# A hybrid decoder step on one core: a ragged tile spread over four row strips, and expert rows gathered at another pace

## The chip, the cores and the metric

The kernel runs on one core of a Trainium2 chip. The metric is the device time of one execution in microseconds, median of three runs. A profiled execution is kept beside them; its rows name the engines PE (TensorE, with PEld for its weight loads), DVE (VectorE), ACT (ScalarE), POOL (GpSimd) and SP (SyncE).

## The reference, cut to what matters

One layer of a decoder over 336 tokens: 256 prompt tokens, 8 sequences of 8 new tokens, and 16 meta tokens that stand ahead of the prompt.

```
proj = rmsnorm(x) @ w_in + b_in
... Conformer branch: GLU, depthwise conv of width 31, layernorm, silu, @ w_conf_out
... Mamba-2 branch: depthwise conv of width 4, then for each chunk of a segment
    acs   = cumsum(dt * A)
    y     = (C B^T * exp(acs_t - acs_s), causal) @ (dt * x)  +  C h * exp(acs)
    h_new = exp(acs_last) * h + B^T @ (exp(acs_last - acs) * dt * x)
... gated group norm over 8 groups, @ w_m_out
x = x + (g_a * y_a + g_b * y_b) @ w_o
# product-key experts, for each token and each of 8 heads
s1, i1 = top_k(q1 @ keys1, 16);  s2, i2 = top_k(q2 @ keys2, 16)
sc, f  = top_k(all 256 sums s1 + s2, 16);  ids = 128 * i1[f // 16] + i2[f % 16]
w      = softmax(sc) * gelu(U[ids] . x)
x      = x + sum over the 128 picks of w * V[ids]
```

Segments are the 16 meta tokens, two chunks of 128 prompt tokens, and each sequence's 8 tokens. The outputs are the normed tokens and the new caches and states.

## The kernel before, in words

**Projections.** Tokens stand along the free dimension (`T` = 336, `T2` = 320 without the meta tokens). Each block of 128 output features is three times eight matmuls over a split of weight and activation into a high and a low part (`proj`, L159 for every recorded matmul `mm`). `weight` fetches 512 KB on the SP queue, ACT makes the high part `wh` and POOL the low part `wl`.

**State-space groups.** There are eight groups; `ssd(g, ...)` is a generator whose steps are run between the projections of the next group by a list written out by hand, and the order on TensorE is that of the program (`keep_in_program_order`). Tokens are cut into three tiles (`TILES`): two prompt chunks of 128, and one tile of 80 rows: eight sequences of 8 rows and the 16 meta rows. `turn` transposes a tile of x and B, `inner` makes the scores of a tile within itself, `state` the running prompt state (for the meta tokens from rows 64 to 80), `running` the part that comes from the old states, `out` sums up a half of the features, and `update` adds to the eight sequences' states in `st`: B is multiplied by four masks (`Bm`), 32 rows hold four sequences, and each of two calls makes four matmuls of 32 rows into two PSUM banks (one of tag `misc`, one of tag `pj`). A group's sum of squares is brought to row g of an eight-row PSUM tile by a stationary of 8 columns from `gsel` (`pgn`).

**Expert stage.** 16 projections `w_q` give queries; for each the scores `psc` of three token tiles (`KTILES`: 128, 128 and 64 tokens) are matmuls with the query as the stationary operand. DVE sorts them (`top16`), tile 0 first. Tile 0 and the 8 last sample tokens get their expert rows by indirect DMA: `gather` brings one row of U and V (8 KB) for each of 128 partitions into one of five buffers `wuv`; 136 such gathers make 136 picks, each a dot product (L1207), two ACT steps and a weighted sum (L1215). The other 184 tokens are done densely: 128 blocks of U (`u_block`, L1284, 16 recorded matmuls a block) and then 128 blocks of V (`v_block`, L1378), 512 KB each on the SP queue, through a ring of eight slots. Between them `g_step` (one-hot matmuls, L1312) scatters the softmax weights.

**Order in that stage.** `Feed` deals tasks out over the blocks: sorting tasks of tiles 1 and 2 and picks over the first `SB` = 84 U blocks, then picks and one-hot steps. `NU` = (42, 28, 37) says how many picks go to U blocks 0 to 83, to the other 44, and to V blocks 0 to 63; the rest goes to the last V blocks. `place` transposes the sorted places of tile 1 and tile 2 on TensorE; `PLACE` = (38, 50) are the U blocks behind which they may stand. Here the order on the engines is the scheduler's, but for such bounds. A gather waits for an earlier block through a list:

```
steps = ustep[SB:] + vstep
if len(steps) > LEAD:
    tc.add_manual_dep(i_.ins, steps[-1 - LEAD], ...Sync...)
```

`ustep` and `vstep` name the first or last matmul of the blocks written so far and `LEAD` is 4, so gathers written among the first 84 U blocks wait for no block.

Of the kernel before, what the change touches and what calls it, by code (L numbers as in the profile page):

```python
# [22 lines left out]
PJ = 512  # L23
# [32 lines left out]
NU = (42, 28, 37)  # L56
# [9 lines left out]
PLACE = (38, 50)  # L66
# [34 lines left out]
NCK = CST["tri"][0]  # L101
NCM = CST["suf"][0]


def constants():
    c = np.zeros((128, NCST), np.float32)

    def put(name, a):
        o, n = CST[name]
        c[:a.shape[0], o:o + n] = a  # L110

    i = np.arange(128)
    put("ident", np.eye(128))
    put("tri", i[:, None] <= i[None, :])
    put("suf", i[:, None] > i[None, :])
    s = np.concatenate([np.arange(64) // 8, np.full(16, 8)])
    j = np.arange(80)
    same = s[:, None] == s[None, :]
    put("tri3", same & (j[:, None] <= j[None, :]))
    put("suf3", same & (j[:, None] > j[None, :]))  # L120
    put("seg", s[:, None] == np.arange(9)[None, :])
    put("segs", i[:, None] % 32 // 8 == np.arange(4)[None, :])
    put("gsel", np.broadcast_to(np.eye(8).reshape(1, 64), (128, 64)))
    for q in range(NQ):
        for t in range(TS):
            c[32 * (q % 4) + 8 * (q // 4) + t, CST["selq"][0] + 8 * q + t] = 1.0
    put("ones", np.ones((128, 128)))
    put("iota128", np.broadcast_to(np.arange(128), (128, 128)))
    put("sel32", i[:, None] % 32 == np.arange(32)[None, :])
    put("sel16", i[:, None] % 16 == np.arange(16)[None, :])  # L130
    put("sel8", i[:, None] % 8 == np.arange(8)[None, :])
    return c


def causal():
    m = np.zeros((128, T), np.float32)
    i, j = np.arange(128), np.arange(80)
    s = np.where(j < 64, j // 8, 8)
    m[:80, 256:] = np.where((s[:, None] == s[None, :]) & (j[:, None] <= j[None, :]), 0.0, -1e30)
    for t0 in (0, 128):  # L140
        m[:, t0:t0 + 128] = np.where(i[:, None] <= i[None, :], 0.0, -1e30)
    return m


def body(tc, ia, oa, stop=None):
    nc = tc.nc
    with ExitStack() as top:
# [220 lines left out]
        dt = dp.tile([H, T], F32, name="dt")  # L368
        dta = dp.tile([H, T], F32, name="dta")
# [39 lines left out]

        def step_sizes():  # L410
# [4 lines left out]
            nc.vector.tensor_scalar(dta, dt, aexp, -1.0, op0=OP.mult, op1=OP.mult)  # L415
            yield
            for i, (t0, L) in enumerate(TILES):
                p = ps.tile([128, 2 * H], F32, name="pdt2", tag="y", bufs=2) if i == 0 else misc([128, 2 * H], "pdt2")
                tr(p[:L, :H], dt[:, t0:t0 + L], ident[:H, :H])
                tr(p[:L, H:], dta[:, t0:t0 + L], ident[:H, :H])  # L420
                dk = mp.tile([128, 2 * H], F32, name=f"dtok{i}")
                nc.scalar.copy(dk[:L], p[:L])
                dtok.append(dk)
# [4 lines left out]
            for i, (t0, L) in enumerate(TILES):  # L428
                tri = C("tri") if i else C("tri3", L)
                suf = C("suf") if i else C("suf3", L)  # L430
                dk = dtok[i]
                mm(pT[:, t0:t0 + L], dk[:L, H:], tri, start=True, stop=True)
                mm(p2[:L, i, 0], tri, dk[:L, H:], start=True, stop=True)
                mm(p2[:L, i, 1], suf, dk[:L, H:], start=True, stop=True)
                if i == 0:
                    sg = C("seg", L)
                    for q in range(9):
                        mm(p3[:, q], sg[:, q:q + 1].to_broadcast([L, 128]), dk[:L, H:], start=True, stop=True)
# [4 lines left out]
            nc.vector.memset(at_[:, 0], 0.0)  # L443
            for L, r_ in ((TILES[0][1], slice(0, 1)), (128, slice(1, 3))):
                nc.vector.tensor_scalar(at_[:L, r_], p2[:L, r_, 0], -1.0, None, op0=OP.mult)
                act(wt_[:L, r_], p2[:L, r_, 1], AF.Exp)
# [136 lines left out]
        def ssd(g, xg, bc, sz):  # L583
# [27 lines left out]
            def turn(i):  # L611
                t0, L = TILES[i]
# [4 lines left out]
                nc.scalar.copy(x_[:L, 256:], p[:L, 256:])  # L617
                nc.vector.tensor_tensor(r4(x_[:L, :256]), r4(p[:L, :256]),
                                        dtok[i][:L, 4 * g:4 * g + 4, None].to_broadcast([L, 4, P]), op=OP.mult)
                w_ = sp.tile([128, 4, P], F32, name=f"wx{i}")  # L620
                nc.gpsimd.tensor_tensor(w_[:L], r4(x_[:L, :256]),
                                        wd[i][:L, 4 * g:4 * g + 4, None].to_broadcast([L, 4, P]), op=OP.mult)
                xt.append(x_)
                wx.append(w_.rearrange("p r c -> p (r c)"))

            def inner(i):
                t0, L = OTILES[i]
                p = misc([128, 128], "pcb")
                mm(p[:L, :L], BT[:, t0:t0 + L], CT[:, t0:t0 + L], start=True, stop=True)
                dv = dec[:L, :, t0:t0 + L]  # L630
                nc.vector.tensor_tensor(dv, dv, p[:L, None, :L].to_broadcast([L, 4, L]), op=OP.mult)

            def state(i):
                rows_ = slice(64, 80) if i == 0 else slice(0, 128)
# [20 lines left out]
            def out(b):  # L655
# [3 lines left out]
                for i, (t0, L) in enumerate(OTILES):  # L659
                    for r in (2 * b, 2 * b + 1):  # L660
                        s = slice((r % 2) * 64, (r % 2) * 64 + 64)
                        mm(py[s, t0:t0 + L], xt[i][:L, r * P:(r + 1) * P], dec[:L, r, t0:t0 + L],
                                         start=True, stop=True)
# [11 lines left out]
            def update(q):  # L675
                pair_ = [misc([128, 512], "pst2"), ps.tile([128, PJ], F32, name="pst2", tag="pj", bufs=3)]
                for d_ in range(2):
                    for s_ in range(2):
                        t_ = slice(32 * s_, 32 * s_ + 32)
                        mm(pair_[s_][:, d_ * 256:(d_ + 1) * 256], Bm[t_, q + d_], wx[0][t_], start=True, stop=True)  # L680
                for s_ in range(2):
                    sv = st[:, 4 * s_ + q:4 * s_ + q + 2].rearrange("p q c -> p (q c)")
                    nc.vector.tensor_tensor(sv, sv, pair_[s_], op=OP.add)

            decay(0)
# [15 lines left out]
            inner(0)  # L701
            yield
# [5 lines left out]
            Bm = sp.tile([S0, 4, N], F32, name="Bm")  # L708
            for r in range(4):
                nc.scalar.activation(Bm[:, r], xt[0][:S0, 256:], AF.Copy, scale=C("segs", S0)[:, r:r + 1])  # L710
# [7 lines left out]
            update(0)  # L718
            yield
# [4 lines left out]
            update(2)  # L724
            nc.sync.dma_start(oa["ssm_s"][g], st)
            yield
            p = pj2("pgn")[:G]
            mm(p, C("gsel")[:, g * G:(g + 1) * G], sq[0], start=True, stop=True)
            if g == 0:
                nc.vector.tensor_copy(pgn, p)  # L730
            else:
                nc.vector.tensor_tensor(pgn, pgn, p, op=OP.add)
# [360 lines left out]
        def gather(c):  # L1093
# [3 lines left out]
            steps = ustep[SB:] + vstep  # L1097
# [10 lines left out]

        for j in range(16):
# [3 lines left out]
            qT = qp.tile([128, T], F32, name="qT", bufs=3)  # L1113
            nc.scalar.copy(qT[:, :T2], p[:, :T2])
            p = misc([128, 3, NK], "psc")
            for i, (t0, L) in enumerate(KTILES):
                nc.tensor.matmul(p[:L, i], qT[:, t0:t0 + L], keys[:, j, :], start=True, stop=True)
# [394 lines left out]
```

## Time and profile before

| | us |
|---|---|
| median of three runs | 1330.94 (1330.91 to 1332.9) |
| the profiled execution | 1334.54 |
| its span, first to last instruction | 1332.8 |

Shares are of the span. A row of a group of instructions reads: line, engine, operation, output<-inputs, shape, count, then busy time, mean of one in ns, and the engine's idle time ahead of it with what ended it. A shape such as 16*128 on a matmul is the rows and columns of the array that it takes. A row of the timeline begins with start and length in us.

### The profile page before, as it was taken

The numbers are of one execution on the slowest core, as the hardware profiler recorded it, in microseconds if no ns is written. First come the engines' busy times: TensorE is split into PE (matmuls) and PEld (weight loads), VectorE is DVE, ScalarE is ACT, GpSimd is POOL, SyncE is SP. The second block draws the span as 40 slices with busy tenths as digits, with TensorE's granted clock in tenths as the row PEclk, the third lists the DMA queues.
The fourth block names the chain that finished last, engine by engine and source line by source line (L and its number), as shares of the span: only waits on it lengthen the run. The fifth ranks groups of instructions, "written<-read, shape, count | busy, mean of one in ns | idle before, by whom it ended". The sixth has DMA issues, their size and how long they took to land.

```text
span 1332.8 us, 23897 instructions
## 1 busy us (share of the span) xinstructions
PE 1294.1 (97%) x9004; PEld 1225.6 (92%) x9004; DVE 993.7 (75%) x2324; ACT 524.5 (39%) x1377; POOL 583.1 (44%) x484
## 2 busy tenths in 40 slices
PE   9999999999999999999999898999999999999997
PEld 7888888888888999988999898999999999999997
DVE  7888778877877335799999987458977888644453
ACT  6777777777765444433322221121210111101012
POOL 2477767876684666744222252032332323122210
PEclk9999999999999999999999999999999999999999
DMA  6434453454434344637999999799999999999992
GB/s 242 161 127 170 166 172 129 153 180 150 157 99 159 129 156 143 210 114 277 381 414 415 377 397 414 282 416 413 396 413 414 415 414 416 398 395 415 414 413 107
DMA packets 85892, 373.68 MB, mean 280 GB/s; under 512 B 9984, under 2 KB 15488, under 8 KB 66192
## 3 DMA queue, kind: packets, MB, share of 16 engines
q1 hardware_dynamic: 65024, 227.52, 46.5%
q0 software_dynamic: 19584, 142.62, 26.2%
q10 hardware_dynamic: 1168, 2.02, 0.4%
q8 instruction: 71, 1.16, 0.3%
q14 instruction: 45, 0.37, 0.1%
HBM read 359.05 MB, written 13.06 MB: 279 GB/s over the span
## 4 chain that ended last, share of the span: by engine, by line
PE 73%; DVE 17%; DMA 7%; ACT 2%; issue 1%; POOL 0%; DVEq 0%; ACTq 0%; POOLq 0%
PE pj L159 29%; PE va L1378 21%; PE pj L1284 12%; DMA eraw<-in_uT_dram 3%; DMA eraw<-in_vE_dram 3%; DVE ygat L1215 2%; DVE wuv L1207 2%; PE pst L159 2%; PE pg L1312 1%; PE po L159 1%; PE py L159 1%; DVE pcv L482 1%; PE pdec L159 1%; DVE cand L1060 1%; PE ptr L164 1%
## 5 line engine op out<-in xcount | busy, mean ns | idle before, releaser
L1095 POOL DMA_INDIRECT wuv<-in_peer_uv_dram,gid x136 | 184.2, 1354 | 490.9 <-PE va L1378 151.6
L1284 PE MATMUL pj<-nd,eraw 128*128 128x184 f32 x2048 | 332.6, 323 | 8.7 <-DMA eraw<-in_uT_dram 5.2
L1284 PEld LDWEIGHTS pj<-nd,eraw 128*128 128x128 f32 x2048 | 321.9, 191 | 11.3 <-ACT S L1286 6.9
L227 POOL TENSOR_TENSOR wl<-wraw,wh 128x1024 fp32r<-128x1024 f32 x111 | 267.2, 2408 | 148.2 <-ACT wh L226 77.3
L1378 PE MATMUL va<-S,eraw 128*128 128x184 f32 x2048 | 326.7, 320 | 2.7 <-DMA eraw<-in_vE_dram 2.6
L1378 PEld LDWEIGHTS va<-S,eraw 128*128 128x128 f32 x2048 | 318.8, 190 | 5.9 <-DMA eraw<-in_vE_dram 4.1
L159 PE MATMUL pj<-ah,wh 128*128 128x336 f32 (+1 forms) x768 | 242.5, 327 | 0.7 <-ACT xnf L202 0.7
L159 PE MATMUL pj<-al,wh 128*128 128x336 f32 (+1 forms) x768 | 233.0, 317 | 0.0
L1215 DVE SCALAR_TENSOR_TENSOR ygat<-wuv,scg,ygat 128x1024 f32<-128x1024 f32 x128 | 164.0, 1281 | 52.2 <-ACT scg L1210 50.5
L1207 DVE SCALAR_TENSOR_TENSOR wuv<-wuv,x2m 128x1024 f32<-128x1024 f32 x128 | 156.0, 1219 | 62.8 <-DMA wuv<-in_peer_uv_dram,gid 62.8
L1209 ACT ACTIVATE scg<-scg 128x1 f32<-128x1 f32 x136 | 27.5, 202 | 403.7 <-DVE wuv L1207 403.4
L226 ACT CAST wh<-wraw 128x1024 fp32r<-128x1024 f32 x125 | 131.2, 1050 | 115.2 <-PE pj L159 70.1
L482 DVE SCALAR_TENSOR_TENSOR pcv<-ccat,vec,pcv 128x256 f32<-128x256 f32 x464 | 148.7, 379 | 17.1 <-ACT pcv L480 17.1
L159 PEld LDWEIGHTS pj<-ah,wh 128*128 128x128 f32 x768 | 146.3, 191 | 8.7 <-ACT xnf L202 2.8
L159 PEld LDWEIGHTS pj<-al,wh 128*128 128x128 f32 x768 | 145.8, 191 | 0.7
L159 PE MATMUL pj<-ah,wl 128*128 128x336 f32 (+1 forms) x768 | 136.8, 315 | 1.3 <-DVE wl L227 1.3
L159 PEld LDWEIGHTS pj<-ah,wl 128*128 128x128 f32 x768 | 119.5, 188 | 2.7 <-DVE wl L227 1.6
L1286 ACT ACTIVATE S<-pj 128x184 f32<-128x184 f32 x128 | 38.7, 319 | 140.2 <-PE pj L1284 140.1
L496 DVE SCALAR_TENSOR_TENSOR pj<-mcat,vec,pj 128x360 f32<-128x360 f32 x96 | 56.3, 587 | 3.7 <-ACT pj L494 3.7
L1319 DVE SCALAR_TENSOR_TENSOR S<-pg,S 128x352 f32<-128x352 f32 (+1 forms) x69 | 33.2, 508 | 32.7 <-PE pg L1312 30.4
L202 ACT ACT_TABLE_LOAD x39 | 50.0, 1283 | 0.7
L1210 ACT ACTIVATE scg<-scg,ggw 128x1 f32<-128x1 f32 x136 | 40.0, 294 | 4.3
(365 smaller groups left out, 1645.1 us busy)
## 6 DMA issues: line engine op xcount, KB each, us to landing
eraw<-in_uT_dram SPq DMA_DIRECT2D x128, 512.0 KB
eraw<-in_vE_dram SPq DMA_DIRECT2D x128, 512.0 KB
wraw<-in_w_in_dram SPq DMA_DIRECT2D x80, 512.0 KB
st<-in_state_dram SPq DMA_DIRECT2D x8, 1024.0 KB
out_ssm_s_dram<-st SPq DMA_DIRECT2D x8, 1024.0 KB
wraw<-in_w_mo_dram SPq DMA_DIRECT2D x16, 512.0 KB
wraw<-in_w_q_dram SPq DMA_DIRECT2D x16, 512.0 KB
wraw<-in_w_co_dram SPq DMA_DIRECT2D x8, 512.0 KB
```

The source lines that it names most:

```text
L159: i_ = nc.tensor.matmul(*a_, **kw)
L202: i_ = nc.scalar.activation(out, in_, f, **kw)
L226: (nc.vector.tensor_copy if on_dve else nc.scalar.copy)(h, src)
L227: (nc.gpsimd if on_pool else nc.vector).tensor_tensor(l, src, h.bitcast(F32), op=OP.subtract)
L482: t = nc.vector.scalar_tensor_tensor(o, i_, wv, a_, op0=OP.mult, op1=OP.add)
L496: nc.vector.scalar_tensor_tensor(o, cat[:, w:w + n], wv, o, op0=OP.mult, op1=OP.add)
L1095: i_ = nc.gpsimd.indirect_dma_start(out=u, out_offset=None, in_=ia["peer_uv"], in_offset=bass.IndirectOffsetOnAxis(ap=gid[:, c:c + 1], axi ...
L1207: nc.vector.scalar_tensor_tensor(u[:, :D], u[:, :D], 1.0, x2m if c < NPICK else x2e, op0=OP.mult, op1=OP.mult, accum_out=w)
L1210: nc.scalar.activation(w, w, AF.Copy, scale=ggw[:, c:c + 1])
L1215: nc.vector.scalar_tensor_tensor(a_, u[:, D:], scg[:, c:c + 1], a_, op0=OP.mult, op1=OP.add)
L1284: i_ = nc.tensor.matmul(p[:, :ND], raw[:, k, :], nd[:, k, :], start=(k == 0), stop=(k == KD - 1))
L1378: i_ = nc.tensor.matmul(va[k // 2][:, k % 2], raw[:, k, :], Sv(b), start=False, stop=(b == 127), skip_group_check=True)
```

## The change

It has two halves. In the state-space groups the tile of 80 rows is laid out over 128 rows: four strips of 32 partitions hold 16 sample rows (two sequences) each and the last strip's upper half holds the 16 meta rows; the rows between are masked in the constants. `spread_in` fills the spread tile `spr` from the transposed data with a ScalarE and a GpSimd copy (a VectorE one for the step sizes), `chunk` picks it for tile 0. All matmuls over that tile then take 128 rows, three masks stand in `Bm` (the third for the meta rows), and `update` is called once, for four strips into four PSUM banks. `gsel` becomes a strip of 135 columns, so that the group-norm sum has a stationary of 128 columns. In the expert stage the third score tile takes 128 columns of a query tile that is padded with zeros, gathers written among the first U blocks wait for a block too, `NU` becomes (46, 26, 36) and `PLACE` (42, 55).

```diff
-NU = (42, 28, 37)
+NU = (46, 26, 36)
-PLACE = (38, 50)
+PLACE = (42, 55)
...
+        def spread_in(c0, n, src, rows=128, copy=nc.scalar.copy):
+            d = spr[:rows, c0:c0 + n]
+            copy(d.rearrange("p c (s i) -> p c s i", i=32)[:, :, :, :16], src[:, :, SQ:T2].rearrange("p c (s i) -> p c s i", i=16))
+            nc.gpsimd.tensor_copy(d[:, :, 112:], src[:, :, T2:])
+
+        def chunk(v, i, c_):
+            return v[:, TILES[i][0]:TILES[i][0] + 128] if i else spr[:v.shape[0], c_]
...
-                for c_, src in enumerate((xg[:, 0, t0:t0 + L], xg[:, 1, t0:t0 + L], BT[:, t0:t0 + L])):
-                    tr(p[:L, c_ * 128:(c_ + 1) * 128], src, ident)
+                for c_, src in enumerate((xg[:, 0], xg[:, 1], BT)):
+                    tr(p[:, c_ * 128:(c_ + 1) * 128], chunk(src, i, c_), ident)
...
-                mm(p, xt[i][rows_, 256:], wx[i][rows_], start=True, stop=True)
+                mm(p, xt[i][:, 256:] if i else Bm[:, 2], wx[i], start=True, stop=True)
...
-            def update(q):
-                pair_ = [misc([128, 512], "pst2"), ps.tile([128, PJ], F32, name="pst2", tag="pj", bufs=3)]
-                for d_ in range(2):
-                    for s_ in range(2):
+            def update():
+                four = [f() for _ in range(2) for f in (
+                    lambda: misc([128, 512], "pst2"), lambda: ps.tile([128, PJ], F32, name="pst2", tag="pj", bufs=3))]
+                for r in range(2):
+                    for s_ in range(4):
                         t_ = slice(32 * s_, 32 * s_ + 32)
-                        mm(pair_[s_][:, d_ * 256:(d_ + 1) * 256], Bm[t_, q + d_], wx[0][t_], start=True, stop=True)
+                        mm(four[s_][:, r * 256:(r + 1) * 256], Bm[t_, r], wx[0][t_], start=True, stop=True)
...
+            spread_in(0, 2, xg)
+            spread_in(2, 1, bc[:, 0:1])
             decay(0)
...
-            p = pj2("pgn")[:G]
-            mm(p, C("gsel")[:, g * G:(g + 1) * G], sq[0], start=True, stop=True)
+            p = pj2("pgn")
+            mm(p, C("gsel")[:, 7 - g:135 - g], sq[0], start=True, stop=True)
...
-            steps = ustep[SB:] + vstep
+            steps = ustep + vstep
...
-            qT = qp.tile([128, T], F32, name="qT", bufs=3)
+            qT = qTs[j % 3]
...
-                nc.tensor.matmul(p[:L, i], qT[:, t0:t0 + L], keys[:, j, :], start=True, stop=True)
+                nc.tensor.matmul(p[:, i], qT[:, t0:t0 + 128], keys[:, j, :], start=True, stop=True)
```

Left out are the constants (573 columns behind the first 440 become 819), `step_sizes`, whose tile 0 takes 128 rows in the same way, and the place of `Bm`, which moves ahead of `state(0)`.

More of the change, by code (lines that the diff above doesn't have):

```diff
@@ L100, with strips @@
 NCST = _cst_layout()
-NCK = CST["tri"][0]
-NCM = CST["suf"][0]
+NCK = CST["segs"][0]
+NCM = CST["tri"][0]
+def strips():
+    p = np.arange(128)
+    j = 16 * (p // 32) + p % 32
+    return j, (p % 32 < 16) | (p >= 112), np.concatenate([np.arange(64) // 8, np.full(16, 8)])
 def constants():
@@ L115, in constants @@
     put("suf", i[:, None] > i[None, :])
[L116 to L123, printed above, removed]
+    j, own, s = strips()
+    n = np.arange(80)
+    own = own[:, None]
+    put("tri3", own & (s[j][:, None] == s[j][None, :]) & (j[:, None] <= j[None, :]))
+    put("tri3n", own & (s[j][:, None] == s[None, :]) & (j[:, None] <= n[None, :]))
+    put("suf3", own & (s[j][:, None] == s[j][None, :]) & (j[:, None] > j[None, :]))
+    put("seg", own & (s[j][:, None] == np.arange(9)[None, :]))
+    put("segs", own & (np.where(j < 64, j // 8 % 2, 2)[:, None] == np.arange(3)[None, :]))
+    put("gsel", np.broadcast_to(np.arange(135) == 7, (128, 135)))
     for q in range(NQ):
@@ L136, in causal @@
     m = np.zeros((128, T), np.float32)
-    i, j = np.arange(128), np.arange(80)
-    s = np.where(j < 64, j // 8, 8)
-    m[:80, 256:] = np.where((s[:, None] == s[None, :]) & (j[:, None] <= j[None, :]), 0.0, -1e30)
+    i, n = np.arange(128), np.arange(80)
+    j, own, s = strips()
+    m[:, 256:] = np.where(own[:, None] & (s[j][:, None] == s[None, :]) & (j[:, None] <= n[None, :]), 0.0, -1e30)
     for t0 in (0, 128):
@@ L367, in body @@
         aexp = mp.tile([H, 1], F32, name="aexp")
-        dt = dp.tile([H, T], F32, name="dt")
-        dta = dp.tile([H, T], F32, name="dta")
+        dtp = dp.tile([H, 2, T], F32, name="dt")
+        dt, dta = dtp[:, 0], dtp[:, 1]
         for k in range(KD):
@@ L408, in body @@
         el = mp.tile([128, 11, H], F32, name="el")
+        spr = mp.tile([128, 3, 128], F32, name="spr")
+        nc.gpsimd.memset(spr, 0.0)
+        def spread_in(c0, n, src, rows=128, copy=nc.scalar.copy):
[4 more added lines that the diff above has]
+            return v[:, TILES[i][0]:TILES[i][0] + 128] if i else spr[:v.shape[0], c_]
         def step_sizes():
@@ L415, in step_sizes @@
             nc.vector.tensor_scalar(dta, dt, aexp, -1.0, op0=OP.mult, op1=OP.mult)
+            spread_in(0, 2, dtp, H, nc.vector.tensor_copy)
             yield
-            for i, (t0, L) in enumerate(TILES):
+            for i in range(3):
                 p = ps.tile([128, 2 * H], F32, name="pdt2", tag="y", bufs=2) if i == 0 else misc([128, 2 * H], "pdt2")
-                tr(p[:L, :H], dt[:, t0:t0 + L], ident[:H, :H])
-                tr(p[:L, H:], dta[:, t0:t0 + L], ident[:H, :H])
+                tr(p[:, :H], chunk(dtp[:, 0], i, 0), ident[:H, :H])
+                tr(p[:, H:], chunk(dtp[:, 1], i, 1), ident[:H, :H])
                 dk = mp.tile([128, 2 * H], F32, name=f"dtok{i}")
-                nc.scalar.copy(dk[:L], p[:L])
+                nc.scalar.copy(dk, p)
                 dtok.append(dk)
@@ L442, in step_sizes @@
             wt_ = mp.tile([128, 3, H], F32, name="wd")
[L443 to L446, printed above, removed]
+            nc.vector.tensor_scalar(at_, p2[:, :, 0], -1.0, None, op0=OP.mult)
+            act(wt_, p2[:, :, 1], AF.Exp)
             act(el, p3, AF.Exp)
@@ L628, in inner @@
                 p = misc([128, 128], "pcb")
[L629 to L631 removed]
+                mm(p[:, :L], chunk(BT, i, 2), CT[:, t0:t0 + L], start=True, stop=True)
+                dv = dec[:, :, t0:t0 + L]
+                nc.vector.tensor_tensor(dv, dv, p[:, None, :L].to_broadcast([128, 4, L]), op=OP.mult)
             def state(i):
[L634 removed]
                 p = misc([128, 256], "pst")
[L636 removed]
+                mm(p, xt[i][:, 256:] if i else Bm[:, 2], wx[i], start=True, stop=True)
                 h_ = sp.tile([128, 256], F32, name=f"hs{i}", bufs=1 + (i == 2))
@@ L661, in out @@
                         s = slice((r % 2) * 64, (r % 2) * 64 + 64)
-                        mm(py[s, t0:t0 + L], xt[i][:L, r * P:(r + 1) * P], dec[:L, r, t0:t0 + L],
+                        mm(py[s, t0:t0 + L], xt[i][:, r * P:(r + 1) * P], dec[:, r, t0:t0 + L],
                                          start=True, stop=True)
@@ L673, in out @@
                 nc.gpsimd.tensor_tensor(y, y, sz[:, b, :], op=OP.mult)
-            def update(q):
-                pair_ = [misc([128, 512], "pst2"), ps.tile([128, PJ], F32, name="pst2", tag="pj", bufs=3)]
-                for d_ in range(2):
-                    for s_ in range(2):
-                        t_ = slice(32 * s_, 32 * s_ + 32)
-                        mm(pair_[s_][:, d_ * 256:(d_ + 1) * 256], Bm[t_, q + d_], wx[0][t_], start=True, stop=True)
-                for s_ in range(2):
-                    sv = st[:, 4 * s_ + q:4 * s_ + q + 2].rearrange("p q c -> p (q c)")
-                    nc.vector.tensor_tensor(sv, sv, pair_[s_], op=OP.add)
+            def update():
[3 more added lines that the diff above has]
+                    for s_ in range(4):
+                        t_ = slice(32 * s_, 32 * s_ + 32)
+                        mm(four[s_][:, r * 256:(r + 1) * 256], Bm[t_, r], wx[0][t_], start=True, stop=True)
+                for s_ in (1, 3, 0, 2):
+                    sv = st[:, 2 * s_:2 * s_ + 2].rearrange("p q c -> p (q c)")
+                    nc.vector.tensor_tensor(sv, sv, four[s_], op=OP.add)
+            spread_in(0, 2, xg)
+            spread_in(2, 1, bc[:, 0:1])
             decay(0)
@@ L701, in ssd @@
             inner(0)
+            Bm = sp.tile([128, 3, N], F32, name="Bm")
+            for r in (2, 0, 1):
+                nc.scalar.activation(Bm[:, r], xt[0][:, 256:], AF.Copy, scale=C("segs")[:, r:r + 1])
             yield
@@ L707, in ssd @@
             state(1)
-            Bm = sp.tile([S0, 4, N], F32, name="Bm")
-            for r in range(4):
-                nc.scalar.activation(Bm[:, r], xt[0][:S0, 256:], AF.Copy, scale=C("segs", S0)[:, r:r + 1])
             yield
@@ L723, in ssd @@
             nc.gpsimd.tensor_tensor(sq[0], sq[0], sq[1], op=OP.add)
-            update(2)
+            update()
             nc.sync.dma_start(oa["ssm_s"][g], st)
             yield
-            p = pj2("pgn")[:G]
-            mm(p, C("gsel")[:, g * G:(g + 1) * G], sq[0], start=True, stop=True)
+            p = pj2("pgn")
+            mm(p, C("gsel")[:, 7 - g:135 - g], sq[0], start=True, stop=True)
             if g == 0:
-                nc.vector.tensor_copy(pgn, p)
+                nc.vector.tensor_copy(pgn, p[:G])
             else:
-                nc.vector.tensor_tensor(pgn, pgn, p, op=OP.add)
+                nc.vector.tensor_tensor(pgn, pgn, p[:G], op=OP.add)
             ygf.append(xg)
@@ L1107, in ahead @@
                     pend[i_] = gather(COLS[i_])
+        qTs = [qp.tile([128, 384], F32, name=f"qT{i}") for i in range(3)]
+        for t in qTs:
+            nc.gpsimd.memset(t[:, T2:], 0.0)
         for j in range(16):
```

29 lines of the change are left out of this document (12 added, 17 removed).

## The prediction

> **What bounds the kernel now.** I read, in this order, the engines' busy times on the page, a table of stretches that I cut at the stage borders, the matmuls of one group in order of time, and the expert stage in order of time.
>
> ```profile
> PE 1294.1 (97%) x9004; PEld 1225.6 (92%) x9004; DVE 993.7 (75%) x2324; ACT 524.5 (39%) x1377; POOL 583.1 (44%) x484
> ...
> q0 software_dynamic: 19584, 142.62, 26.2%
> ...
> L1215 DVE SCALAR_TENSOR_TENSOR ygat<-wuv,scg,ygat 128x1024 f32<-128x1024 f32 x128 | 164.0, 1281 | 52.2 <-ACT scg L1210 50.5
> L1207 DVE SCALAR_TENSOR_TENSOR wuv<-wuv,x2m 128x1024 f32<-128x1024 f32 x128 | 156.0, 1219 | 62.8 <-DMA wuv<-in_peer_uv_dram,gid 62.8
> ```
> ```profile
> 56.00:400.00 344.00, 339.27 (x2369) 299.06 (x2368) 273.95 (x727) 263.39 (x682) 250.43 (x244) 1.00 0.46 154
> 400.00:566.00 166.00, 163.37 (x1095) 160.49 (x1095) 92.56 (x107) 82.25 (x126) 103.02 (x53) 0.99 0.48 159
> 566.00:615.00 49.00, 47.54 (x320) 44.51 (x319) 46.93 (x235) 18.42 (x49) 23.09 (x13) 1.00 0.40 132
> 615.00:648.00 33.00, 29.82 (x171) 26.71 (x170) 32.34 (x154) 10.87 (x40) 11.98 (x12) 0.95 0.98 392
> 648.00:858.00 210.00, 198.43 (x1335) 195.46 (x1334) 185.63 (x487) 48.65 (x171) 54.15 (x38) 0.99 0.98 386
> 858.00:980.00 122.00, 119.83 (x964) 118.13 (x963) 89.54 (x149) 23.89 (x88) 38.35 (x26) 1.00 0.99 397
> 980.00:1161.00 181.00, 178.30 (x1411) 173.38 (x1411) 148.10 (x253) 21.74 (x85) 49.20 (x37) 1.00 1.02 414
> 1161.00:1321.00 160.00, 160.00 (x1028) 160.00 (x1028) 73.35 (x96) 17.64 (x63) 33.08 (x27) 1.00 0.92 370
> ```
> The columns after the length are PE, PEld, DVE, ACT and POOL busy, the granted clock, the DMA share and GB/s. TensorE is the bound from 56 to 566: 339 of 344 us busy while DVE (274), ACT (263), POOL (250) and DMA (0.46) have room. From 566 DVE is full too (46.93 of 49, then 32.34 of 33). From 615 DMA is full as well: 0.98 to 1.02 of its time. So what is taken from TensorE before 566 is time won, and what is taken from it later is won only where DMA and DVE let it.
>
> **The change, part by part.**
>
> **1. The sample and meta tile over four strips, and the widened stationary of the group norm.** One group's small matmuls, in order of time:
>
> ```profile
> 152.02 1.39 PE L159 MATMUL pj<-ah,wl 128*128 128x336 f32 x8
> 153.34 1.07 PE L159 MATMUL pq<-st,gs 128*32 128x256 f32 x16
> 154.35 0.33 PE L159 MATMUL pcb<-bc 128*64 128x64 f32 x2
> ...
> 157.18 1.39 PE L159 MATMUL pj<-ah,wl 128*128 128x336 f32 x8
> 158.41 0.38 PE L159 MATMUL pcb<-bc 128*128 128x128 f32 x2
> 158.72 0.69 PE L159 MATMUL pst<-wx,xt 16*128 16x256 f32 x2
> 159.34 0.42 PE L159 MATMUL pj<-ah,wh 128*128 128x336 f32 x1
> ...
> 167.52 0.59 PE L159 MATMUL pst<-wx,xt 128*128 128x256 f32 x2
> 168.04 0.92 PE L159 MATMUL py<-dec,xt 64*64 64x64 f32 x12
> ...
> 178.50 1.13 PE L159 MATMUL pst<-wx,Bm 32*128 32x256 f32 x8
> 179.56 0.31 PE L159 MATMUL pdec<-acs,id 96*128 96x320 bf16 x1
> ...
> 188.37 1.39 PE L159 MATMUL pj<-ah,wl 128*128 128x336 f32 x8
> 189.69 0.71 PE L159 MATMUL pgn<-sq,cstm 128*8 128x320 f32 x2
> 190.33 0.44 PE L164 MATMUL ptr<-cst,xg 128*128 128x128 f32 x2
> ```
> Matmuls overlap, so I go from start to start. The same eight matmuls take 1.23 us when the next has the same shape (157.18 to 158.41) and 1.32 when it has fewer columns (152.02 to 153.34, 188.37 to 189.69). A change of tile shape thus costs 0.09 us, entering and leaving. Per group:
> - State update: two batches of four matmuls (eight records, 178.50 to 179.56) cost 1.06 us each and 0.09 to enter, 2.30 together. Afterwards there is one batch of sixteen records in four row strips. The trace has no four row strips; nearest is pq, sixteen records of the same 256 columns in four column strips: 1.01, and 0.09 to enter. Win 1.20. Bounds: if only two strips overlap, as now, the batch takes 2.0 and the win is one entry, 0.1; better than pq I don't assume. I take 1.20, since pq has the same count, width and number of strips.
> - Meta state: 16 rows become 128. 0.31 before it and 0.62 in it, against 0.22 and 0.43 for the full one (0.52 from 167.52 to 168.04, less the 0.09 to leave): 0.28.
> - Group-norm sum, 8 columns become 128: two shape changes go, 0.18. Score of the tile (154.35), 64 rows become 128: one change, 0.09. In each of two output steps the change between 64*64 and 128*64 goes: 0.18.
>
> Sum 1.93 us, times 8 groups: 15.4.
>
> [...] No run here shows row strips yet.
>
> Added work: two ScalarE and two GpSimd copies a group fill the strips and one of four masks goes. At about 0.4 us an ACT instruction of this size (the masks, below), that is 0.4 us more of ACT in a 43 us group; ACT and POOL have 80 and 94 us free in the 344. It is hidden unless a transpose waits for a copy; a projection of 24 matmuls (3.7 us at 1.23 for eight) lies between. The moved second update also brings its output DMA forward a step; SP has nothing waiting on it that is late.
>
> ```profile
> L710 ACT ACTIVATE Bm<-xt,cstm 64x128 f32<-64x128 f32 x32 | 11.1, 407 | 0.0
> ```
> ```profile
> PE pst L159 <- DVE dec L631: 2.6, 1, 2.6
> ```
> One wait sits in the last group (378 us): TensorE waits for DVE there, so it loses what it won in that group, 2 us. Taken: 13.5, bounds 5 (strips overlap by two only, and some copies late) and 15.4. The start pays for 246 more columns of constants, 0.13 MB, and two copies ahead of the first transposes: 0 to 1 us, taken as 0, because the weights are already queued ahead of them.
>
> **2. Wide third score tile.**
>
> ```profile
> L1117 PE MATMUL psc<-keys,qT 128*64 128x128 f32 x32 | 6.7, 296 | 2.0 <-ACT sall L1119 1.9
> ```
> Sixteen tiles, two shape changes each at 0.09: 2.9 us, bounds 0 and 3.5. This stretch (566 to 648) is also full on DVE, which then opens the gathers; TensorE's win brings DVE's input forward, not its end. I take 2. Three memsets of 64 columns on POOL go unseen: it is half idle there.
>
> **3. Gathers, deal and transposes.**
>
> ```profile
> 728.16 0.33 PE L1177 MATMUL pix<-cst,pick 128*128 128x128 f32 x1 [2.47 <-DVE pick L1061]
> ...
> 763.85 0.27 PE L1177 MATMUL pix<-cst,pick 64*128 64x64 f32 x1 [2.81 <-DVE pick L1061]
> ...
> 818.09 2.73 PE L1284 MATMUL pj<-nd,eraw 128*128 128x184 f32 x16 [1.07 <-DMA eraw<-in_uT_dram]
> 820.65 0.64 PE L1312 MATMUL pg<-oh 128*128 128x64 f16 x16
> 821.86 2.73 PE L1284 MATMUL pj<-nd,eraw 128*128 128x184 f32 x16 [0.57 <-DMA eraw<-in_uT_dram]
> ```
> ```profile
> 861.13 0.94 POOL L1095 DMA_INDIRECT wuv<-in_peer_uv_dram,gid  x1 [31.33 <-PE pj L1284]
> ```
> ```profile
> 838.00:862.00 24.00, 23.99 (x179) 23.57 (x178) 12.91 (x23) 4.19 (x15) 0.87 (x1) 1.00 0.73 258
> ```
> ```profile
> L1312 PE MATMUL pg<-oh 128*128 128x64 f16 x736 | 30.6, 193 | 0.3 <-DVE oh L1308 0.2
> ```
> Undisturbed, 1028 matmuls take 160.00 us (1161 to 1321): 2.49 us a block of 16. From 648 to 1161 there are 184 blocks, 458 us; 46 one-hot steps (736 records by 16) of 0.57 us, 26; the load of the accumulators 2.5: 487 of 513. So 26 us are stalls, all before 1161. A gather is 142.62 MB by 136, 1.05 MB, 2.53 us at 414 GB/s; a block of 0.52 MB is 1.27; together 3.80, and 818.09 to 821.86 is 3.77: there each block shares the queues with one gather. The picture: once DVE has its sorting behind it (the second wait for it ends at 763.85) picks run at DVE's own pace, their gathers starve blocks such as those at 818 to 822, and then the gathers wait 31 us for a block of the second part while DMA runs at 258 GB/s: a hole of 24 x (1 - 258/414) = 9 us.
>
> With the wait on a U block, gathers of the first part come one to 84/46 = 1.83 blocks; that needs 1.83 x 1.27 + 2.53 = 4.85 us of DMA against 4.55 of TensorE, so DMA stays full and the hole closes. POOL has nothing but gathers behind the new wait; behind a late gather stands DVE's pick (2.5 us from the two rows above), in order. Four more picks are 10 us of DVE in the first part, 185.63 of 210 busy: it fits.
>
> How much can come? DMA moves 0.386 x 210 + 0.397 x 122 + 0.414 x 181 = 204 MB from 648 to 1161, 493 us at 414 GB/s, and one gather more is dealt ahead of that border (29 left instead of 30): 496. So no more than 17 of the 26 us can go, whatever the waits. The transposes behind blocks 42 and 55 instead of 38 and 50 have 10 to 12 us more for DVE; the waits ahead of them (2.47 and 2.81) go unless the four picks, up to 10 us, come ahead of the sorting. Moving gathers from the later parts (28 to 26, 37 to 36) takes 5 and 2.5 us of DMA from stretches that stall. I take 12; bounds 17 and -6 (a transpose that waits 10 us once, against some of the hole).
>
> **Sum.** 13.5 + 2 + 12 = 27.5 us. The profiled execution took 1334.54 us (span 1332.8), 3.6 above the median; the win is a difference inside that execution and I take it off the median: 1330.94 - 27.5 = 1303.4, say 1303.
>
> **The rivals.**
> - **The transfers decide (0.20).** Nothing comes out of part 3: the same bytes pass a DMA that is already full, the hole is filled by gathers that only make blocks late elsewhere. For it: 0.98 to 1.02 in every stretch to 1161. Against: the hole of 9 us is real and TensorE idles in its neighbourhood. Price: 10 of the 12 us, about 1313. [...]
> - **Banks or copies hold TensorE in the groups (0.11).** The update now holds four banks until DVE has added them, and the next projection but one needs one. Four adds of 0.68 us end 2.7 us after the batch, a projection lasts 3.7; so DVE may be 1 us late for free. The row below has DVE idle ahead of 12 of 32 adds, which speaks against it. At 1 us a group it costs 8: about 1311. [...]
>
> ```profile
> DVE st L683 <- PE pst L159: 11.0, 12, 1.8
> ```
> - **Everything comes (0.08).** 15.4 + 3.5 + 17 and a lesser wait at 378: about 1294.
> - **Slower (0.06).** DVE reaches a paced gather that has not landed, with the rest of the second sort queued behind it, and TensorE, in order, stands at the transposes of block 55. It decides from the point where that wait passes parts 1 and 2: 16 us, six picks of 2.5 us ahead of the sort. At 20 us: about 1335. Against: the two waits for DVE's sort are now under 3 us each, and 10 to 12 us of delay are granted.
>
> **How the numbers follow.** The forecast has 0.55, 1303 with its own range 1296 to 1309. A difference of 0.2% (2.7 us) is about what a measurement tells from none. Range 1291 to 1319: up to the first two rivals together (1321) but one or two us, down to "everything". Slower by 0.2% only in the last rival, 0.05; in between 0.02; faster 0.93.
>
> **What would show it.** Part 1: one batch of sixteen pst records of about 1.0 us a group, no 16*128, 128*8 or 128*64 pcb rows, and the 56 to 400 stretch some 13 us shorter. Part 2: no 128*64 score rows. Part 3: no 31 us wait of POOL, DMA near 400 GB/s throughout the first part, gathers every 4.5 us after the sort, and under 15 us of stalls where there were 26. Wrong if the batch takes 2 us, if waits for ACT or POOL copies appear at the transposes, or if TensorE's waits move to the later transposes.

## The result, and the profile after

The changed kernel took 1310.32 us, median of four runs (1308.83 to 1312.94), beside 1331.3 for the kernel before on the same chip: a ratio of 0.9842, 95% interval 0.9822 to 0.9863. That is 21 us less; forecast were 27.5, and 1303 with a range from 1291 to 1319. The profiled execution is the slowest of the four, 1312.94 with a span of 1311.1.

The same stretches as ahead of the prediction, cut at the new stage borders (columns as there):

```profile
56.00:390.00 334.00, 327.42 (x2378) 298.84 (x2376) 273.78 (x734) 262.20 (x689) 254.55 (x260) 0.99 0.45 160
390.00:553.00 163.00, 160.91 (x1091) 159.02 (x1092) 90.56 (x104) 81.45 (x124) 103.32 (x56) 1.00 0.47 162
553.00:600.00 47.00, 45.54 (x323) 45.04 (x322) 46.14 (x232) 18.65 (x50) 22.96 (x13) 1.00 0.40 140
600.00:633.00 33.00, 27.32 (x168) 24.95 (x167) 31.52 (x153) 10.82 (x39) 11.69 (x12) 1.00 0.99 388
633.00:840.00 207.00, 198.85 (x1341) 196.14 (x1340) 183.90 (x488) 47.16 (x169) 56.69 (x41) 0.99 1.00 399
840.00:962.00 122.00, 122.00 (x976) 120.32 (x975) 98.79 (x161) 25.18 (x97) 36.94 (x26) 1.00 1.02 414
962.00:1141.00 179.00, 176.59 (x1402) 172.19 (x1401) 143.37 (x248) 20.53 (x80) 45.06 (x35) 1.00 1.01 409
```

From 600 on DMA is full, at 399 and 414 GB/s from 633 to 962 where before had 386 and 397: the hole is filled. TensorE is busy throughout from 840 to 962: 44 U blocks at 2.49 us, 15 one-hot steps at 0.57 and 2.5 for the accumulators make 121 of these 122 us. Where the 21 us come from is read best from the first start of an instruction of each stage in the two traces (us):

| first start of | before | after | stage, before | stage, after | won |
|---|---|---|---|---|---|
| pq, first group | 68.6 | 71.9 | | | -3.3 |
| Conformer output, after the groups | 395.0 | 385.1 | 326.4 | 313.2 | 13.2 |
| first score psc | 557.8 | 545.8 | 162.8 | 160.7 | 2.1 |
| first U block | 615.3 | 600.6 | 57.5 | 54.8 | 2.7 |
| U block 84 | 858.2 | 840.4 | 242.9 | 239.8 | 3.1 |
| first V block | 982.5 | 962.3 | 124.3 | 121.9 | 2.4 |
| V block 64 | 1161.4 | 1140.8 | 178.9 | 178.5 | 0.4 |
| last matmul's end | 1324.5 | 1303.8 | 163.1 | 163.0 | 0.1 |

The strips won 13.2 us in the groups, the start gave 3.3 back, the score tile won 2.7, and the gathers with the deal 6.0. The other 2.1 fell in the stage of the Conformer output, which the change doesn't touch: the twelve traces with the strips take from 160.4 to 164.6 us there, so these 2.1 are no win of the change. Of the small matmuls, first the update's batch in order of time, then two groups, the meta state and the group-norm sum:

```profile
175.85 1.34 PE L166 MATMUL pj<-ah,wl 128*128 128x320 f32 x8
177.12 1.15 PE L166 MATMUL pst<-wx,Bm 32*128 32x256 f32 x16
178.20 0.31 PE L166 MATMUL pdec<-acs,id 96*128 96x320 bf16 x1
```
```profile
L166 PE MATMUL pst<-wx,Bm 128*128 128x256 f32 x16 | 4.8, 380 | 0.0
L166 PE MATMUL pgn<-sq,cstm 128*128 128x320 f32 x16 | 5.7, 438 | 1.1 <-POOL sq L737 1.1
```

Sixteen records in four row strips take 1.08 us (177.12 to 178.20), where two batches of eight took 2.30 with their entries; the meta state and the group-norm sum are 128*128 now, and one of the sums waits 1.1 us for GpSimd.

### The profile page after: what moved, and what is told of

Its sections match the earlier page's. It is cut to its first block, busy times and chain, and to the rows that moved or that the text cites. A ratio compares the mean times of both kernels' runs of the same rounds, so it can differ in the third digit from the quotient of the medians.

```text
span 1311.1 us, 23940 instructions
## 1 busy us (share of the span) xinstructions
PE 1275.0 (97%) x9004; PEld 1222.7 (93%) x9004; DVE 990.0 (76%) x2323; ACT 520.5 (40%) x1384; POOL 580.4 (44%) x505
## 4 chain that ended last, share of the span: by engine, by line
PE 74%; DVE 16%; DMA 6%; ACT 2%; POOL 1%; issue 1%; DVEq 0%; ACTq 0%; POOLq 0%
PE pj L166 28%; PE va L1395 22%; PE pj L1301 15%; DMA eraw<-in_vE_dram 3%; DMA eraw<-in_uT_dram 2%; DVE wuv L1224 2%; DVE ygat L1232 2%; PE pg L1329 1%; DVE pcv L497 1%; PE pst L166 1%; PE po L166 1%; PE pdec L166 1%; PE py L166 1%; DMA wuv<-in_peer_uv_dram,gid 1%; DVE si L1031 1%
## 5 line engine op out<-in xcount | busy, mean ns | idle before, releaser
L1109 POOL DMA_INDIRECT wuv<-in_peer_uv_dram,gid x136 | 177.8, 1307 | 491.3 <-PE va L1395 113.5
```

The lines of the kernel that those rows point to most:

```text
L1109: i_ = nc.gpsimd.indirect_dma_start(out=u, out_offset=None, in_=ia["peer_uv"], in_offset=bass.IndirectOffsetOnAxis(ap=gid[:, c:c + 1], axi ...
```

## The experiments

**The halves.** Strips alone (the deal, the pace, the places of the transposes and the score tile as before):

```diff
-NU = (46, 26, 36); PLACE = (42, 55); steps = ustep + vstep
+NU = (42, 28, 37); PLACE = (38, 50); steps = ustep[SB:] + vstep
-            qT = qTs[j % 3]
+            qT = qp.tile([128, T], F32, name="qT", bufs=3)
...
```


> The four strips alone: the deal, the pace, the later transposes and the wide score tile are as before. My theory (strips won 13 us over the groups and lost 3 at the start): 1320 to 1322 us, and the sixteen update records take 1.08 us in each group as in the changed kernel. Rival (the strips' 10 us are partly given back because the expert stage, which starts earlier, is bound by its transfers): 1324 or more, with more stalls between the first U block and the end than the kernel before has. Rival (part 3 brought nothing, all 21 us come from the strips): 1312 or less.

Measured: 1320.51 us, ratio 0.9899 (0.988 to 0.9918). The stretch from the first U block to the end takes 708.9 us (709.2 before), the groups 312.9, the score tile's stage 57.5 again: nothing of the strips is given back later.

The expert half alone: the kernel before with `NU = (46, 26, 36)`, `PLACE = (42, 55)`, `steps = ustep + vstep` and the wide score tile:

> The expert half alone (wide third score tile, deal 46, 26, 36, the pace behind U blocks, transposes at 42 and 55); the groups are as before. My theory: about 2.7 us from the score tile and 6 from the rest, so 1321 to 1324 us; together with the strips' 10 this makes the 21 us of the whole. Rival (the two halves help each other): 1326 or more, and the sum of both halves alone is under 18 us.

Measured: 1322.38, ratio 0.9924 (0.9909 to 0.9939). The two ratios make 13.4 and 10.1 us, 23.5 together against 21.0 for the whole, whose interval is 2.7 us to each side: within the intervals the halves add up. Of this kernel only the time is read, not the stages.

**Does the strips' win hang on the order of the matmuls?**

```diff
-                for r in range(2):
-                    for s_ in range(4):
+                for s_ in range(4):
+                    for r in range(2):
```


> The changed kernel with the two loops of the update swapped: the two matmuls of one strip stand one behind the other, so that neighbours on TensorE use the same strip. If overlap of neighbouring strips is what pays, the batch of sixteen records goes from 1.08 to about 1.9 us (only one pair in two overlaps), some 6 to 7 us over eight groups: 1316 to 1318. If the batch is bound by something else (the four banks, or the issue of sixteen records), the batch stays within 0.1 us of 1.08 and the time at 1310.

Measured: 1309.91, ratio 0.9824 (0.9807 to 0.9841), and the batch takes 1.10 us (174.44 to 175.54) beside 1.08 in the changed kernel:

```profile
174.44 1.17 PE L166 MATMUL pst<-wx,Bm 32*128 32x256 f32 x16
175.54 0.31 PE L166 MATMUL pdec<-acs,id 96*128 96x320 bf16 x1
```
```profile
L166 PE MATMUL pst<-wx,Bm 32*128 32x256 f32 x128 | 9.3, 400 | 0.0
```

The mean of a record, 400 ns, says nothing here: it is 400 in the kernel before too, whose 128 records are busy for 18.1 us in all and not 9.3. The theory of neighbours is out: two matmuls of one strip in succession don't hold up the next strip.

**Deal and pace.** The changed kernel without the pace (`steps = ustep[SB:] + vstep`), with the old deal (`NU = (42, 28, 37)`), and with both:

> The changed kernel without the pace: gathers dealt to the first 84 U blocks wait for no block. The prediction's theory (the pace closes the hole): POOL waits about 30 us for a block again near U block 84, DMA has a hole, and the time is 6 to 9 us longer (1316 to 1320). My theory now (the pace binds only from gather 41 on, because VectorE is behind it until then, so that it only spreads the last five gathers): 0 to 3 us longer (1310 to 1313).

> The changed kernel with the old deal 42, 28, 37, pace and transposes kept. Theory (the deal only moves bytes between stretches in which DMA is full): 1309 to 1312, the stretch to block 84 some 4 us shorter, those behind it some 4 us longer. Rival (the deal is what closed the hole; with four picks fewer ahead of block 84 the gathers wait again): 1314 to 1318, and a wait of POOL of over 15 us for a U block.

> The changed kernel with the old deal 42, 28, 37 and without the pace: strips, wide score tile and later transposes stay. With the runs of the deal (42, 28, 37 with the pace: 1304) and without the pace (46, 26, 36: 1312.8) this fills the square of deal and pace. Theory (pace and old deal fit together, each alone is worth little): 1315 to 1318, that is the strips' kernel at 1320.5 less 3 for the score tile. Rival (the old deal is simply the better one, with or without the pace): 1304 to 1308.

Measured (median us, ratio to before with its interval):

| deal | without the pace | with the pace |
|---|---|---|
| 42, 28, 37 | 1319.89, 0.9895 (0.9875 to 0.9915) | 1304.02, 0.9793 (0.9772 to 0.9813) |
| 46, 26, 36 | 1312.82, 0.9851 (0.9833 to 0.9869) | 1310.32, 0.9842 (0.9822 to 0.9863) |

With the old deal the pace is worth 15.9 us, with the new one 2.5, which these intervals don't tell from nothing; and once the pace is there, the new deal costs 6.3. The first of the three came out as my later theory had it (0 to 3 us longer), not as the prediction did. For the second both ranges were wrong (1309 to 1312 and 1314 to 1318, against 1304.02). The third is 2 us above its theory's 1315 to 1318. The stretches around U block 84, and POOL's longest wait for U blocks, show why. First the old deal without the pace, then with it, then the changed kernel, and last the new deal without the pace:

```profile
785.00:815.00 30.00, 25.89 (x213) 24.96 (x211) 24.72 (x40) 5.68 (x21) 9.40 (x7) 1.00 1.02 416
815.00:845.00 30.00, 27.35 (x209) 26.40 (x209) 18.49 (x30) 5.52 (x20) 0.00 (x0) 1.00 0.85 322
```
```profile
POOL wuv L1109 <- PE pj L1301: 68.4, 12, 37.8
```
```profile
782.00:812.00 30.00, 29.29 (x236) 28.69 (x235) 19.43 (x33) 5.49 (x21) 5.37 (x5) 1.00 1.02 413
812.00:842.00 30.00, 30.00 (x257) 29.59 (x257) 25.72 (x44) 5.98 (x23) 8.40 (x6) 1.00 1.02 413
```
```profile
785.00:815.00 30.00, 26.86 (x218) 25.92 (x217) 20.24 (x33) 5.04 (x20) 5.87 (x6) 1.00 1.02 414
815.00:845.00 30.00, 30.00 (x243) 29.65 (x242) 22.53 (x38) 5.94 (x23) 7.92 (x6) 1.00 1.02 415
```
```profile
POOL wuv L1109 <- PE pj L1301: 40.8, 13, 7.2
```
```profile
815.00:845.00 30.00, 28.96 (x230) 28.31 (x229) 22.31 (x34) 6.07 (x24) 5.21 (x4) 1.00 1.02 412
```
```profile
POOL wuv L1109 <- PE pj L1301: 21.0, 8, 4.1
```

The hole of the kernel before stands in the first pair: POOL issues nothing for 30 us (it waits 37.8 us for one U block) and DMA falls to 322 GB/s. The pace closes it (second pair). The deal of 46 closes it too, without the pace (412 GB/s, no wait over 4.1 us): it has four gathers more to issue ahead of block 84. Having both buys the same thing twice. What the new deal costs lies ahead of it, from the first U block to block 84 (239.8 us in the changed kernel, 229.4 with the old deal and the pace): in the changed kernel DMA falls to 355 GB/s while VectorE sorts and TensorE stands once for ScalarE, and then it stands at every block of the burst of gathers that follows (the stretches of the changed kernel and of the old deal with the pace; then blocks of the changed kernel):

```profile
725.00:755.00 30.00, 28.33 (x170) 28.13 (x171) 28.67 (x70) 9.04 (x30) 11.61 (x7) 0.94 0.92 355
```
```profile
722.00:752.00 30.00, 30.00 (x194) 29.72 (x194) 28.00 (x61) 9.31 (x30) 8.33 (x7) 1.00 0.99 382
```
```profile
726.67 6.62 PE L1301 MATMUL pj<-nd,eraw 128*128 128x184 f32 x30 [2.63 <-ACT S L1303]
```
```profile
780.77 2.73 PE L1301 MATMUL pj<-nd,eraw 128*128 128x184 f32 x16 [1.03 <-DMA eraw<-in_uT_dram]
784.54 2.73 PE L1301 MATMUL pj<-nd,eraw 128*128 128x184 f32 x16 [1.04 <-DMA eraw<-in_uT_dram]
```

780.77 to 784.54 is 3.77 us for a block, as before the change. Between the first six U blocks and the last one, eight blocks take over 3.3 us in the changed kernel, 15 with the old deal and no pace, one with the old deal and the pace.

Earlier transposes (`PLACE = (38, 50)`, the rest as changed):

> The changed kernel with the transposes back behind blocks 38 and 50. Theory of the prediction (TensorE waits there for VectorE's sort, and this wait is time): two waits of 2 to 3 us each at the transposes appear again and the time is 4 to 5 us longer, 1314 to 1316. Rival (a wait at a transpose lets block and gather transfers run ahead, and fewer stalls follow): the waits appear, but the time stays within 1.5 us of 1310.

Measured: 1311.65, ratio 0.9846 (0.9827 to 0.9866). The rival: the waits are there,

```profile
PE pix L1194 <- DVE pick L1075: 5.1, 2, 3.7
```

and from the first U block to the end it takes 702.6 us against 703.2. From 722 to 752, where TensorE is busy for 25.44 of 30 us, the DMA share is 0.98. From 600 on TensorE waits for U blocks for 1.2 us in all, beside 5.5 in the changed kernel, and the starved blocks of 780 are gone. The later transposes win nothing by themselves.

A tighter pace (among the first 84 U blocks a gather waits for the block just before it, not for the one four before):

```diff
-            if len(steps) > LEAD:
-                tc.add_manual_dep(i_.ins, steps[-1 - LEAD], ...
+            lead = 0 if len(steps) <= SB else LEAD
+            if len(steps) > lead:
+                tc.add_manual_dep(i_.ins, steps[-1 - lead], ...
```


> The changed kernel with a tighter pace: a gather dealt to the first 84 U blocks waits for the block just before it in the deal and not for the one four before. My theory (the pace is too loose to bind while VectorE is behind, so its burst of a gather every 3.0 us starves blocks 62 to 68): the tighter pace binds earlier, the starved blocks become fewer, and the time is 2 to 5 us shorter, 1305 to 1308. Rival (the late gathers are VectorE's backlog, which a tighter pace only makes later): 1310 to 1314, with the starved blocks just as many or further on.

Measured: 1307.11, ratio 0.9807 (0.9789 to 0.9825). The median is 3.2 us lower, but the intervals overlap. The starved blocks of the burst come later (67 to 71 instead of 63 to 68) and are hardly fewer, so the reason I gave is not borne out.

Three gathers moved from U blocks 84 to 127 into the last 64 V blocks (`NU = (42, 25, 37)`), and the same with the tighter pace:

> The changed kernel with the deal 42, 25, 37: against the deal 42, 28, 37 three gathers more move from U blocks 84 to 127 to the last 64 V blocks, where DMA is at 0.88. Theory (from the first U block to V block 64 the transfers decide, and a gather taken out of it is 2.5 us): 7 us less than with 42, 28, 37, so 1296 to 1298 us, and the seven starved blocks at the first V blocks (3.76 us each) gone or fewer. Rival (the burst at the first V blocks is VectorE's backlog and comes back elsewhere, or the last blocks now starve): 1301 to 1306.

> The deal 42, 25, 37 and the tighter pace together. Theory (both take gathers away from starved blocks): no more than 2 us below the deal alone, 1294 to 1298, since with 42 picks the pace binds already. Rival (with 42 picks the tighter pace only makes gathers late, and DMA has holes): 2 us or more above the deal alone.

Measured: 1299.84, ratio 0.9756 (0.974 to 0.9772), and 1306.88, ratio 0.9799 (0.9779 to 0.982). The first is the fastest version of the study, 10.5 us below the changed kernel, 2 to 4 above my theory; its interval just touches that of 42, 28, 37 (0.9772). The first and second half of the V blocks, first of this deal, then of 42, 28, 37:

```profile
950.00:1125.00 175.00, 174.88 (x1399) 171.53 (x1398) 143.01 (x246) 20.40 (x80) 44.61 (x36) 1.00 1.02 414
1125.00:1292.00 167.00, 163.67 (x1040) 161.57 (x1038) 83.64 (x111) 20.76 (x76) 32.26 (x29) 1.00 0.92 373
```
```profile
949.00:1130.00 181.00, 175.89 (x1395) 171.05 (x1394) 144.92 (x249) 20.57 (x81) 48.66 (x37) 1.00 1.02 414
1130.00:1293.00 163.00, 162.75 (x1042) 161.93 (x1040) 78.49 (x104) 19.90 (x72) 29.21 (x27) 1.00 0.91 367
```

Up to V block 64 the time falls by 6.5 us (from 532.0 to 525.5 behind the first U block), 2.2 for each of three gathers at an unchanged 414 GB/s; the last blocks, now with 32 gathers, stall for 3.7. That makes 2.8 of the 4.2 us between the medians; the profiled executions lie only 1.6 apart (1300.55 and 1302.13), in part because the stage of the Conformer output, which the deal doesn't touch, is 2.4 longer in the first. The six starved blocks among the first seven V blocks (over 3.3 us with 42, 28, 37) are gone. The tighter pace costs 7 us on top. In its trace 6 of them are in the V part, whose halves take 179.3 and 168.3 us (174.9 and 166.7 without it). That fits the rival, by which it only makes gathers late with 42 picks; what holds them up in the V part, where the pace is the old one, isn't shown.

**The start.** The rows of VectorE, GpSimd and TensorE at 50 us, of the changed kernel and then of the kernel with swapped update loops, whose instructions up to here are the same:

```profile
50.99 2.57 DVE L245 CAST acs<-s3r 32x336 bf16<-32x336 f32 x1
...
54.09 0.67 DVE L497 SCALAR_TENSOR_TENSOR pcv<-ccat,vec,pcv 128x64 f32<-128x64 f32 x2
```
```profile
50.97 2.41 POOL L234 TENSOR_TENSOR wl<-wraw,wh 128x1024 fp32r<-128x1024 f32 x1 [2.93 <-ACT wh L233]
...
53.72 2.71 POOL L234 TENSOR_TENSOR wl<-wraw,wh 128x1024 fp32r<-128x1024 f32 x1
```
```profile
60.63 0.30 PE L166 MATMUL pdec<-acs,id 96*128 96x320 bf16 x1 [1.77 <-ACT dec L209]
...
62.44 0.48 PE L166 MATMUL pj<-ah,wh 128*128 128x336 f32 x1
62.72 0.48 PE L166 MATMUL pj<-al,wh 128*128 128x336 f32 x1
```
```profile
50.43 0.33 DVE L245 CAST acs<-s3r 32x336 bf16<-32x336 f32 x1
```
```profile
51.03 2.55 POOL L234 TENSOR_TENSOR wl<-wraw,wh 128x1024 fp32r<-128x1024 f32 x1 [3.56 <-ACT wh L233]
```

The same cast takes 0.33 us where it begins ahead of GpSimd's subtraction, and 2.57, to just behind the subtraction's end, where it begins 0.02 us behind its start. The change's own VectorE copy at 32 us, beside a subtraction from 32.17 to 34.56, meets the same fate (2.19 us in the changed kernel, 2.20 in that with the old deal and the pace); by ScalarE (in the next kernel) it takes 0.30:

```profile
32.45 2.19 DVE L422 COPY spr<-dt 32x128 f32<-32x128 f32 x1
```
```profile
31.48 0.30 ACT L421 COPY spr<-dt 32x128 f32<-32x128 f32 x1
```

VectorE has next to no idle time there (19.91 of 20 us busy from 35 to 55), so the decay of the first group is late, TensorE waits 1.77 us, and then eleven matmuls start 0.28 us apart instead of 0.154, another 1.4; the granted clock is 0.56 from 62.2 to 65.8. The kernel before isn't free of this either: its next cast is held, and TensorE waits 1.50 us for the same decay,

```profile
49.79 2.28 DVE L453 CAST id<-cst 96x32 bf16<-96x32 f32 x1
```
```profile
58.90 0.30 PE L159 MATMUL pdec<-acs,id 96*128 96x320 bf16 x1 [1.50 <-ACT dec L202]
```

but behind that wait its clock is 1.00 from 62.2 to 65.8. So 1.7 of the start's 3.3 us are the later decay (60.63 against 58.90) and 1.4 the clock.

Of ten profiled executions with both the copy and the cast, four show it (first pq at 71.2 to 71.9), six don't (68.5 to 68.7). The two kinds differ ahead of the cast already: from 41 to 51 us the granted clock is 0.83 in the four, as in the kernel before, and 0.66 in the six. Copy and casts out of GpSimd's way:

```diff
-            spread_in(0, 2, dtp, H, nc.vector.tensor_copy)
+            spread_in(0, 2, dtp, H)
...
-            nc.vector.tensor_tensor(r_, r_, b_, op=OP.subtract)
-            nc.vector.tensor_copy(dst[2 * H:2 * H + n], r_)
+            nc.vector.tensor_tensor(dst[2 * H:2 * H + n], r_, b_, op=OP.subtract)
...
-            keep(nc.vector.tensor_copy(identb, ident))   # likewise id3, mneg
+            nc.scalar.copy(identb, ident)                # one step earlier
```


> The changed kernel with the one-input VectorE copies at the start taken out of the way of GpSimd's subtractions: the step sizes are spread by ScalarE, the last of the three bf16 copies is written by the subtraction itself, and three constant casts move to ScalarE ahead of it. My theory (a one-input copy of VectorE lasts as long as the GpSimd subtraction that runs beside it, 2.2 and 2.6 us instead of 0.3, and these two are the start's loss): no such row over 0.5 us before the first group, TensorE's waits at the first decay matmuls (0.4 and 1.8 us) and the half clock after them gone, and the first pq about 3 us earlier; 1306 to 1308 us. Rival (VectorE is full there anyway with the convolution, so the waits only move to the next thing it makes): the first pq within 1 us of before, and 1309 to 1311 us.

> The deal 42, 25, 37 together with the start of the run before in which the one-input VectorE copies are out of GpSimd's way. Theory (the start loses 3 us only in those executions in which the cast begins just behind a GpSimd subtraction, and without the cast it can't): first pq at 68.7 us or before, and the median up to 2 us below that of the deal alone (1299.8), so 1297.5 to 1300. Rival (the start's 3 us come from the clock or from VectorE's load, not from the cast): the first pq is at 71 to 72 us, with TensorE's wait of 1.8 us at the decay matmuls, in some execution, or the median is no lower than 1300.

Measured: 1311.9, ratio 0.9849 (0.983 to 0.9868), and, with the deal 42, 25, 37, 1303.9, ratio 0.978 (0.9766 to 0.9794). The first pq of the two:

```profile
68.57 1.07 PE L166 MATMUL pq<-st,gs 128*32 128x256 f32 x16
```
```profile
67.61 0.85 PE L166 MATMUL pq<-st,gs 128*32 128x256 f32 x12
```

The first has the clock of the six (0.66 from 41 to 51 us) and is no earlier than they are. The second has that of the four (0.83) and is 4 us ahead of them, earlier than any other trace. So held copies are the loss where the clock is 0.83; that rests on one trace, and what sets the clock there isn't shown. The time is not won, and both of my theories missed it: the second kernel is 4 us above the one without this edit. Its groups take 314.4 us (312.7 there), and the U blocks up to 44 take 126.2 (123.1), all of it at blocks 2 and 3, among the last scores. Why these differ I didn't settle. Kernels that are alike in a stage differ by up to 4 us in it (160.4 to 164.6 for the Conformer output), so smaller steps between medians are not read here.

## Why the prediction was right or wrong

**Part 1, 13.5 us: right in mechanism and size, but for the start.** In the groups the strips won 13.2 us (11.9 to 13.7 in the twelve profiled kernels that have them). The batch took 1.08 us, where by pq's row I took 1.01: the row misses by 0.07. The step that failed is the start, "0 to 1 us, taken as 0": I priced the constants and the copies by their own durations, and not by what a VectorE copy meets on GpSimd, nor by the clock behind a wait. It cost 3.3 us in this execution (1.7 and 1.4 of them), and in six others the first pq is where it was before.

**Part 2, 2 us: right.** 2.7 measured, with the strips alone as the control (57.5 without it, 54.7 with it).

**Part 3, 12 us: mis-sized, 6.0 measured.** The hole was the right picture and the pace the right cure: the old deal shows it, 15.9 us, close to the bound of 17. But two of the signs I named did not come: by my own sum the stalls up to V block 64 are about 20 us (508 less 488), not under 15, and most gathers between 754 and 784 come 3.0 us apart, not 4.5. Two steps failed. I counted the deal as a gain ("takes 5 and 2.5 us of DMA from stretches that stall") and its four picks as free ("it fits"), while my own sum for the first part, 4.85 us of DMA for 4.55 of TensorE, said that 46 gathers there are too many; with 42 it is 84/42 = 2 blocks, 2 x 1.27 + 2.53 = 5.07 against 4.98, nearly even. And I gave the transposes' 5.3 us of waits a share of the gain; with the waits back the time is the same (702.6 us from the first U block to the end, against 703.2), and TensorE waits 1.2 us for U blocks instead of 5.5.

The forecast missed by 6.5 us: part 3 fell 6.0 short and the start cost 3.3. Part 2 gave 0.7 more than forecast, and the stage of the Conformer output 2.1, which is luck.

**The rivals.** "The transfers decide" (1313) came nearer than the forecast: a gather taken out of the stretch up to V block 64 is 2.2 us. But it is wrong that nothing comes of the order of gathers. Where the share is 1 a starved block takes 3.77 us, again; in the hole of the old deal without the pace the share is 0.85, and the pace, which changes the order alone, is worth 15.9 us. "Banks or copies hold TensorE" is not seen: TensorE waits 1.1 us at a group-norm sum and 0.7 for a weight's low part, no transpose waits for a copy, and no projection is listed as waiting for a bank. "Everything comes" (1294) is out: part 3 gave 6.0 of 17. "Slower" is out: no transpose of the sorted places waits at all in the changed kernel.

## What to carry to other kernels

Find the hole before curing it, and cure it once: the two edits that close the same hole here don't add (the pace is worth 15.9 us with the old deal and 2.5 with the new one), and the second one's price stays (6.3). Where a queue is full, count what each stretch has to move against what it can, and move work into the stretch that has room (here the last V blocks: three gathers for 4 us by the medians, 2.8 by the stages). Filling the idle strips was worth 13.2 us in the groups here: price such a change from a batch of the same count and width, and look at what the copies that fill the strips meet on their engine (2.19 us on VectorE beside a subtraction, 0.30 on ScalarE).

## What the runs showed of the hardware

- VectorE copies and casts that began 0.02 to 0.34 us behind the start of a GpSimd subtraction ended only behind its end (2.57 us for 0.33; 2.19, beside 0.30 on ScalarE; 2.28 in the kernel before); where casts came first it was the subtraction that took longer (2.71 and 2.55 us, not 2.41). So it was with `al`, an instruction with two tensor inputs, 0.54 us behind the start: free, then behind a subtraction, and that subtraction, all of the changed kernel:

```profile
517.18 0.54 DVE L936 SCALAR_TENSOR_TENSOR al<-xT,vec,ah 128x320 fp32r<-128x320 f32 x1
522.42 2.21 DVE L936 SCALAR_TENSOR_TENSOR al<-xT,vec,ah 128x320 fp32r<-128x320 f32 x1 [0.63 <-ACT ah L935]
```
```profile
521.88 2.39 POOL L234 TENSOR_TENSOR wl<-wraw,wh 128x1024 fp32r<-128x1024 f32 x1
```

Not held was the convolution (two pcv rows took 0.67 us beside a subtraction, at 54.09, and 0.66 at 50.30, ahead of one). What makes the difference isn't shown.

- After a wait of 1.77 us the granted clock was 0.56 (62.2 to 65.8 us) and eleven matmuls ran at about half their rate (0.28 us apart, not 0.154), so that wait cost nearly twice its length (1.77 and 1.4 us). Behind the kernel before's wait of 1.50 us in the same place it was 1.00; what makes the difference isn't shown.
- Sixteen matmuls in four row strips took about as long as eight in two in the kernel before (1.08 and 1.06 us), so the four strips ran side by side, and with two of a strip in succession as with one of each in turn (1.10 and 1.08).
